# Another order for the last projection's blocks, and the MLP's second weight group in the place of finished rows: an encoder block on one core

## The chip, the core and the metric

The kernel runs on one core of a Trainium2 chip. A core has five engines with their own instruction queues: TensorE (PE) for matmuls, VectorE (DVE), ScalarE (ACT), GpSimd (POOL) and SyncE (SP), whose queue here holds nearly all DMAs. The metric is the time of one execution on the chip in microseconds; lower is better. Three timed runs of the kernel before took 1295.22, 1295.95 and 1296.48 us.

## What is computed

One layer of an encoder block on 1024 tokens of width 1024, in float32: RMSNorm, an input projection, neighbourhood attention and a gated short convolution, each with its own projection back, a gated sum of both called merged, and then these lines of the reference, which the change is about:

```python
x = x + merged @ w_o[l]
h = rms_norm(x, norm2_g[l]) @ w_mlp_in[l]       # 1024 x 4096
x = x + jnp.square(jax.nn.relu(h)) @ w_mlp_out[l]
```

## The kernel before

**Numbers.** Every float32 matmul is made of three fp16 ones: each operand is split into a high half and a low rest ("split" below: ACT copies the high half, DVE subtracts it from the operand), and three of the four products are added. High and low halves of the merged rows lie in tiles `M[0]` (mH) and `M[1]` (mL), the columns of one block of 128 tokens after those of another.

**The projection W_o.** `proj(b, half)` makes block b (128 tokens, eight of them) and half of the 1024 output columns: a group of 24 matmuls into one PSUM bank, then one DVE instruction that scales the bank and adds it into X1. Sixteen such groups; `anybank()` hands out eight banks in turn, so a later group waits for whoever reads the bank of the eighth before it. First come six half 0s (blocks 4, 5, 0, 1, 2, 6), then `built(cO[1])` waits for the weights of half 1, then the pairs: (0,1), (4,1), (1,1), (5,1), (3,0), (7,0), (2,1), (6,1), (3,1), (7,1).

**Pairs.** Blocks n and n+4 are a pair. When both halves of both are in X1, `pair(n)` makes their share of the MLP's input: squares and a reciprocal root for RMSNorm (ACT, DVE), a scaled copy of both blocks into a tile `form` (ACT), four differences and sums of these (`sums`, DVE), the split into `v16` (ACT, DVE), and two DMA transposes on SP's queue into U2[0] (u2T, forms 0 to 3) and U2[1] (u2x, forms 4 to 6).

**The MLP's first product.** It is done in seven products in place of eight (a two-by-two scheme in the manner of Strassen and Winograd), in 16 column groups q. `quad(q)` is one group: seven groups of 12 matmuls, one for each product, in the order 1, 6, 5, 4, 2, 7, 3; behind them the posts, small DVE additions from PSUM into the tile `as` (`post7`, for one, reads the banks of products 7, 4 and 5). Products 1, 2, 5 and 4 read u2T, and 6, 7 and 3 read u2x. Quads 0 and 1 run in two halves of 256 columns (256 tokens of each half of the tokens): first both first halves, which read the columns of pairs 0 and 1, and then both second halves, which read those of pairs 2 and 3. From quad 2 on the width is 512.

**Weights of a group.** For each q two raw tiles come by DMA; ACT scales them (`rows_scaled`, with the norm's gain), squares them for a power-of-two scale, POOL adds four form sums into `tsum` (`forms_sum`), a one-column matmul on PE adds up the squares over the partitions (`all_sum`; its column `ones` comes from DVE), and seven forms are split into fp16 into a tile `w16_1` (`forms_split`). These tiles take turns on three tags (`TAGS`); group 1's, "K", is the memory of the merged rows, so it waits for the last matmul of the projection. The prep of group q+1 starts when group q's split is out (L1206).

**What sets the order.** The program is written by generators: `fg` and `bg` are lists of foreground and background work. After each matmul group `unit(..., steps, ticks)` takes `steps` steps of the foreground and `ticks` steps of the background (L185). `need(q)` forces background until group q is ready. So steps, ticks and `gap`s decide behind which group each instruction stands. Each engine then works through its own queue in that order.

**W2.** After quad 15 the second product (weights again through the raw tiles of the same pool) starts: ACT squares its first weights, DVE reduces, POOL makes the sums of their forms; the squared-ReLU outputs `as` are turned into forms by POOL, stored by SP into HS and loaded again as `hf`.

## Time and profile before

| | us |
|---|---|
| profiled execution | 1298.12 |
| its span | 1296.0 |
| timed runs, median | 1295.95 |
| PE busy | 1217.8 (94% of the span) |
| DVE busy | 940.0 |
| ACT busy | 763.9 |
| POOL busy | 433.7 |

The span is the time from the first to the last instruction of the profiled execution, and all starts below count from it. Busy shares are averages: the projection, the quads and W2 have different limits, and so the prediction reads windows of the span and the waits of PE in them.

### The profile page before, as it was taken

To read this page: it belongs to the slowest core of one execution; us is meant where nothing else is said; L and a number is where in the kernel's file an instruction comes from. 1 tells how busy PE (TensorE), PEld (TensorE's weight loads), DVE (VectorE), ACT (ScalarE), POOL (GpSimd) and SP (SyncE) were. 2 spreads that over 40 slices of the span, in tenths; PEclk is the share of its full clock that TensorE was granted. 3 is DMA by queue.
4 is the path that set the end of the run, shared out by engine and by line. 5 is a ranking of instruction groups with operands and counts; after the bars stand their busy time and mean duration, and the time that the engine had idled before them with its cause. 6 is when DMAs were issued, how large, how long until landed. Compare 5 with 4: busy or idle time off the path is not lost. (4 is left out here: it accounts for less than half of the span.)

```text
span 1296.0 us, 17018 instructions
## 1 busy us (share of the span) xinstructions
PE 1217.8 (94%) x6294; PEld 579.5 (45%) x6294; DVE 940.0 (73%) x1719; ACT 763.9 (59%) x1169; POOL 433.7 (33%) x269
## 2 busy tenths in 40 slices
PE   5999997889999999999997899999996899999998
PEld 4544443444444444444456444444442344444443
DVE  7578767878657686886575476667746588889798
ACT  6777557667564455533665678777774564646430
POOL 2430011111231111100102587667738316080562
PEclk8999999989999999999998999999998899999999
DMA  6558445646552221225284454445462762526112
GB/s 251 125 196 159 106 70 118 132 81 139 113 112 84 65 65 37 70 86 193 63 165 104 147 179 140 151 157 179 170 228 90 240 239 92 234 98 244 67 64 98
DMA packets 170803, 173.35 MB, mean 134 GB/s; under 512 B 131424, under 2 KB 131936, under 8 KB 166624
## 3 DMA queue, kind: packets, MB, share of 16 engines
q1 hardware_dynamic: 170720, 172.27, 44.8%
q8 instruction: 49, 0.80, 0.3%
q14 instruction: 34, 0.28, 0.1%
HBM read 102.51 MB, written 37.75 MB: 108 GB/s over the span
## 5 line engine op out<-in xcount | busy, mean ns | idle before, releaser
L188 PEld LDWEIGHTS <-w 128*128 128x128 f16 x1512 | 149.7, 100 | 161.8 <-issue 9.8
L188 PEld LDWEIGHTS <-ops 128*128 128x128 f16 x1356 | 133.5, 99 | 181.3 <-issue 26.7
L1138 POOL TENSOR_TENSOR as<-as 128x512 f32<-128x512 f32 x64 | 111.7, 1746 | 85.3 <-ACT as L1271 81.6
L854 PE MATMUL ps_d<-uT,w_ws 128*128 128x512 f16 x528 | 128.3, 384 | 2.5 <-ACT w_ws L290 2.4
L188 PE MATMUL ps_s<-ops 128*128 128x512 f16 (+1 forms) x528 | 121.3, 380 | 7.1 <-ACT acc L1487 4.2
L188 PE MATMUL ps_d<-ops 128*128 128x512 f16 x492 | 115.4, 385 | 9.7 <-DVE as L1298 9.7
L188 PEld LDWEIGHTS <-uT 128*128 128x128 f16 x648 | 64.7, 100 | 70.7 <-issue 5.9
L1388 ACT ACTIVATE ops<-hf,sc 128x2048 f16<-128x2048 f32 x26 | 51.8, 1994 | 69.7 <-PE ps_d L188 24.7
L188 PE MATMUL ps_d<-u2T,w 128*128 128x512 f16 (+1 forms) x420 | 89.4, 365 | 3.3 <-DMA u2T<-v 2.9
L971 DVE SCALAR_TENSOR_TENSOR w<-raw,sc,w 128x512 f16<-128x512 f32 (+1 forms) x32 | 40.7, 1272 | 67.7 <-ACT w L977 67.7
L188 PEld LDWEIGHTS <-w_s 128*128 128x128 f16 x588 | 56.7, 98 | 71.3 <-DMA uT<-gs 2.2
L188 PE MATMUL ps_s<-u2x,w 128*128 128x512 f16 (+1 forms) x396 | 85.1, 366 | 3.2 <-DMA u2x<-v 3.2
L1390 DVE SCALAR_TENSOR_TENSOR ops<-hf,sc,ops 128x2048 f16<-128x2048 f32 x26 | 70.7, 2718 | 16.0 <-ACT ops L1388 16.0
L944 ACT ACTIVATE raw<-raw,sc 128x256 f32<-128x256 f32 x184 | 76.0, 494 | 6.1 <-DMA raw<-in_weights 6.1
L188 PE MATMUL ps_o<-ops 128*128 128x512 f16 x336 | 77.5, 380 | 1.4 <-DVE ops L1397 0.8
L958 POOL TENSOR_TENSOR tsum<-raw 128x512 f32<-128x512 f32 x30 | 50.8, 1710 | 81.2 <-ACT raw L944 66.3
L854 PEld LDWEIGHTS <-w_ws 128*128 128x128 f16 x528 | 51.1, 99 | 58.3 <-issue 3.9
L1403 POOL TENSOR_TENSOR raw<-raw 128x1024 f32<-128x1024 f32 x8 | 22.7, 2837 | 140.8 <-DVE ops L1397 140.8
L1269 ACT ACTIVATE as<-as 128x2048 f32<-128x2048 f32 x16 | 30.5, 1909 | 62.9 <-DVE as L1303 62.9
L958 POOL TENSOR_TENSOR gsum<-raw 128x512 f32<-128x512 f32 x14 | 18.5, 1338 | 133.4 <-issue 68.7
L971 DVE SCALAR_TENSOR_TENSOR w<-tsum,sc,w 128x1024 f16<-128x1024 f32 x30 | 61.4, 2087 | 0.0
L278 DVE SCALAR_TENSOR_TENSOR w_ws<-raw,sc,w_ws 128x512 f16<-128x512 f32 (+2 forms) x72 | 51.1, 764 | 3.5 <-ACT w_ws L290 3.5
(300 smaller groups left out, 2526.4 us busy)
## 6 DMA issues: line engine op xcount, KB each, us to landing
raw<-in_weights SPq DMA_DIRECT2D x92, 512.0 KB, 4.0
hs<-as SPq DMA_DIRECT2D x16, 1792.0 KB, 6.9
hf<-hs SPq DMA_DIRECT2D x26, 1024.0 KB, 10.4
w2x<-in_weights SPq DMA_DIRECT2D x16, 512.0 KB, 6.8
raw<-in_weights SPq DMA_DIRECT2D x16, 384.0 KB, 4.0
xt<-in_x SPq DMA_DIRECT2D x8, 512.0 KB, 9.8
gs<-s SPq DMA_DIRECT2D x4, 1024.0 KB, 6.6
x<-in_x SPq DMA_DIRECT2D x8, 512.0 KB, 8.6
```

The costliest lines, as they stand in the source:

```text
L188: T.matmul(ps, l, r, start=a, stop=b)
L278: V.scalar_tensor_tensor(lo, self.raw[p][:, o:o + m], sc[:, c:c + 1], hi, op0=OP.mult, op1=OP.subtract)
L854: T.matmul(ps, l, r, start=a, stop=b)
L944: A.activation(v, v, AF.Copy, scale=sc[:, at(g, 4 * i + k)])
L958: G.tensor_tensor(t[:, o], a, b, op=OP.add)
L971: V.scalar_tensor_tensor(P[:, a:b, 1], w, sc[:, s], P[:, a:b, 0], op0=OP.mult, op1=OP.subtract)
L1138: sub.tensor_tensor(z[o], z[a], z[b], op=op)
L1269: A.activation(f[:, 0:4], f[:, 0:4], AF.Relu)
L1388: A.activation(P[:, 1, 0], hf, AF.Copy, scale=sc[:, Rs])
L1390: V.scalar_tensor_tensor(P[:, 1, 1], hf, sc[:, Rs], P[:, 1, 0], op0=OP.mult, op1=OP.subtract)
L1403: G.tensor_tensor(w11[i2], w11[i2], w12[i2], op=OP.add)
```

## The change

It has five parts.

1. Half 0 of blocks 3 and 7 is moved behind pair 2. Pairs end at groups 8, 10, 12 and 16 in place of 8, 10, 14 and 16. Pair 3's squares are made in two halves, the first right behind (7, 0), and one DVE addition puts them together.
2. Group 1's weights are prepared by a function of their own, `prep_m`: six of the seven forms go into `M[0]`, into columns of blocks 0, 1, 2, 4, 5 and 6, whose groups have all been issued when `m_free` is set; the seventh goes into a small tile `t4`. The four sums are done by POOL in place, in the raw tiles, between the splits. Its work runs beside the projection's end, and group 1 needs no `tsum`. `seven` (its hunk is left out) now also takes a function that says where a form lies.
3. The background runs further ahead: `need(0)` in the projection is gone, ticks behind a half 1 group are 8, the gaps in `sums1` are shorter, and the chain of groups from 2 on follows right behind `prep_m`. From group 2 on, each group's `all_sum` and split stand about half a quad earlier.
4. Quads 0 and 1 take three foreground steps behind each group in place of two.
5. Their second halves run the products in the order 1, 2, 5, 4, 6, 7, 3 (those of u2T first), with post 5 behind post 6.

```diff
         ch.sum = sum_of(sm)
         yield
 
+    def parts(todo, s, then):
+
+        prev = None
+        for n, it in enumerate(todo + [None]):
+            if prev:
+                o, w = prev
+                V.scalar_tensor_tensor(o(1), w, sc[:, s], o(0), op0=OP.mult, op1=OP.subtract)
+                then(n - 1)
+            if it:
+                o, w = it
+                A.activation(o(0), w, AF.Copy, scale=sc[:, s])
+            prev = it
+            yield
+
     def forms_split(ch, t, s, P):
 
+        def then(n):
+            if n == 1:
+                done[0] += 2
+                load_upto(done[0] + 5)
         r = ch.r
         todo = [(0, 1, r[0][:, 0:1]), (1, 3, r[1]), (3, 5, t[:, 0:2]), (5, 7, t[:, 2:4])]
-        prev = None
-        for it in todo + [None]:
-            if prev:
-                a, b, w = prev
-                V.scalar_tensor_tensor(P[:, a:b, 1], w, sc[:, s], P[:, a:b, 0], op0=OP.mult, op1=OP.subtract)
-                if a == 1:
-                    done[0] += 2
-                    load_upto(done[0] + 5)
-            if it:
-                a, b, w = it
-                A.activation(P[:, a:b, 0], w, AF.Copy, scale=sc[:, s])
-            prev = it
-            yield
+        yield from parts([((lambda i, a=a, b=b: P[:, a:b, i]), w) for a, b, w in todo], s, then)
 
     def prep_s(n):
 
...
             sub.tensor_tensor(z[o], z[a], z[b], op=op)
             yield
 
-    pair_done, fv = [0], []
+    pair_done, fv, halves = [0], [], {}
+
+    def squares(n, half=None):
+
+        ss = tmp(2)
+        a, c = (8, slice(0, D)) if half is None else (4, slice(512 * half, 512 * half + 512))
+        for i in range(2):
+            A.activation(SQJ[:, :a], X1[:, n + 4 * i, c].rearrange("p (a t) -> p a t", a=a), AF.Square,
+                         accum_out=sc[:, at(ss, i)])
+        halves.setdefault(n, []).append(ss)
+        yield
 
     def pair(n):
 
-        ss, y = tmp(2), tmp(2)
-        for i in range(2):
-            A.activation(U2[1][:, 0, :, :, 384:512].rearrange("p s k t -> p (s k) t").bitcast(BF16),
-                         X1[:, n + 4 * i].rearrange("p (a t) -> p a t", a=8), AF.Square, accum_out=sc[:, at(ss, i)])
-        yield
-        yield from rstd(ss, D, y, 9)
+        y = tmp(2)
+        if n == 3:
+            yield from squares(3, 1)
+            a, b = halves[3]
+            V.tensor_tensor(sc[:, a], sc[:, a], sc[:, b], op=OP.add)
+        else:
+            yield from squares(n)
+            a = halves[n][0]
+        yield from rstd(a, D, y, 9)
         while pair_done[0] < n:
             yield
         if not n or n == 3:
...
     def sums1(q):
 
         ch = c1[q]
-        while q == 2 and pair_done[0] < 4:
-            yield
         if q == 0:
             tsum[0] = U2[1][:, 2].rearrange("p s k t -> p (s k t)").bitcast(F32).rearrange("p (i c) -> p i c", i=4)
-        elif q % 2:
+        elif q % 2 == 0:
+            while q == 2 and pair_done[0] < 4:
+                yield
             t = wsp.tile([128, 2, 4, 512], F32, name="tsum", tag="ws")
             for i in range(2):
                 tsum[q + i] = t[:, i]
         yield from rows_scaled(ch, g2)
-        yield from forms_sum(ch, tsum[q], 3 if q > 1 else 2 - q)
+        yield from forms_sum(ch, tsum[q], (0, 0, 1)[q] if q < 3 else 3)
 
     def prep1(q):
 
...
         P = P1[q] = pool.tile([128, 7, 2, 512], F16, name="w16_1", tag=tag)
         yield from forms_split(ch, tsum[q], s, P)
         ready.add(q)
-        if 0 < q < 15:
+        if 1 < q < 15:
             yield from sums1(q + 1)
+
+    SQJ = U2[1][:, 0, :, :, 384:512].rearrange("p s k t -> p (s k) t").bitcast(BF16)
+    m_free = [False]
+
+    def prep_m():
+
+        ch = c1[1]
+        yield from rows_scaled(ch, g2)
+        sm = cols_of("prep", 2)
+        for i in range(2):
+            A.activation(SQJ, ch.raw[i].rearrange("p (a t) -> p a t", a=8), AF.Square, accum_out=sc[:, at(sm, i)])
+            yield
+        ch.sum = sum_of(sm)
+        yield
+        s, ch.inv = yield from scale_of(ch.sum, 9, 3)
+        (w11, w12), (w21, w22) = ([ch.raw[i].rearrange("p (n m) -> p n m", n=2)[:, j] for j in range(2)]
+                                  for i in range(2))
+        while not m_free[0]:
+            yield
+        last = w4p.tile([128, 2, 512], F16, name="t4", bufs=1)
+
+        def place(f, n=1):
+            if f == 6:
+                return lambda i: last[:, i].rearrange("p (k c) -> p k c", k=4)
+            k, c = 4 * (f // 3), 128 * (f % 3)
+            return lambda i: M[0][:, k:k + 4, 512 * i + c:512 * i + c + 128]
+
+        def form(w):
+            return w.rearrange("p (k c) -> p k c", k=4)
+
+        def then(n):
+            if n < 4:
+                o, a, b = ((w11, w11, w12), (w12, w12, w22), (w22, w22, w11), (w21, w21, w22))[n]
+                G.tensor_tensor(o, a, b, op=OP.add)
+        yield from parts([(place(f), form(w)) for f, w in ((0, w11), (2, w22), (1, w21))], s,
+                         lambda n: then(n if n < 1 else 1) if n < 2 else (then(2), then(3)))
+        yield from parts([(place(f), form(w)) for f, w in ((3, w11), (4, w12), (5, w22), (6, w21))], s, lambda n: None)
+        done[0] += 2
+        load_upto(done[0] + 5)
+        P1[1] = lambda w, i, k: place(w)(i)[:, k]
+        ready.add(1)
+        yield from sums1(2)
 
 
     push(cO[1])
...
                 post()
         mm = tok_mms(ps, actM, b, cO[half], 8, 512, 0)
         if mms is None:
-            unit(mm, fin, 6, 4 + 2 * (half and b % 4 > 1))
+            unit(mm, fin, 6, 8 if half else 4)
         else:
             mms.append((mm, fin))
 
...
-    bg.extend([sums1(0), prep1(0)])
+    bg.extend([sums1(0), prep1(0), prep_m()])
+    bg.extend(prep1(q) for q in range(2, 16))
     two = []
     for b in (4, 5):
         proj(b, 0, None, two)
...
     for b in (0, 1, 2, 6):
         proj(b, 0)
     built(cO[1])
-    for n in range(4):
-        if n == 2:
-            proj(3, 0)
-            proj(7, 0)
-            need(0)
-            bg.append(sums1(1))
-            for q in range(1, 16):
-                bg.append(prep1(q))
+    for n in range(3):
         proj(n, 1)
         proj(n + 4, 1, lambda n=n: fg.append(pair(n)))
+    m_free[0] = True
+    proj(3, 0)
+    proj(7, 0, lambda: fg.append(squares(3, 0)))
+    proj(3, 1)
+    proj(7, 1, lambda: fg.append(pair(3)))
     pe_done[0] = 0
 
 
...
         ps = {}
         z = [AS[q][:, i, c0:c1] for i in range(7)]
 
+        def post6(ps):
+            V.tensor_tensor(z[5], ps[6], z[4], op=OP.add)
+            if c0:
+                post5(ps)
+
         def post5(ps):
             V.tensor_tensor(z[1], ps[5], z[5], op=OP.subtract)
 
...
                 fg.append(h_done(q))
         seven(P1[q], actU2, c0, c1, {
             1: lambda ps: A.activation(z[4], ps[1], AF.Copy),
-            6: lambda ps: V.tensor_tensor(z[5], ps[6], z[4], op=OP.add),
-            5: post5,
+            6: post6, 5: None if c0 else post5,
             2: lambda ps: V.tensor_tensor(z[0], ps[2], z[4], op=OP.add),
-            7: post7, 3: post3}, 2, 5)
+            7: post7, 3: post3}, 2 if c1 == 512 else 3, 5, (1, 2, 5, 4, 6, 7, 3) if c0 else (1, 6, 5, 4, 2, 7, 3))
 
     def whole(q):
         quad(q)
```

Three places in the instruction order. The first is DVE's queue from the projection's end into quad 0. Before, the last block of X1 (x1, from bank ps_s_6024) comes right behind pair 2's v16 subtractions (v16_5813, L1165), and group 1's split (w16_1_6085) behind that:

```order
L1165 TENSOR_TENSOR v16_5813<-form_5812,v16_5813 128x4x512
L1165 TENSOR_TENSOR v16_5813<-form_5812,v16_5813 128x3x512
L1226 SCALAR_TENSOR_TENSOR x1_5464<-ps_s_6024,sc_71,x1_5464 128x512
L390 TENSOR_SCALAR sc_71<-sc_71 128x2
L971 SCALAR_TENSOR_TENSOR w16_1_6085<-raw_5670,sc_71,w16_1_6085 128x512
L971 SCALAR_TENSOR_TENSOR w16_1_6085<-raw_5676,sc_71,w16_1_6085 128x2x512
L971 SCALAR_TENSOR_TENSOR w16_1_6085<-tsum_5932,sc_71,w16_1_6085 128x2x512 x2
```

Now pair 2's subtractions (v16_5831, L1185) stand among group 1's splits into the merged rows (mH_3618) and the small tile, and the last two blocks of X1 (banks ps_d_6013 and ps_s_6062) behind all of these:

```order
L969 SCALAR_TENSOR_TENSOR mH_3618<-raw_5676,sc_71,mH_3618 128x4x128
L1185 TENSOR_TENSOR v16_5831<-form_5830,v16_5831 128x4x512
L969 SCALAR_TENSOR_TENSOR mH_3618<-raw_5670,sc_71,mH_3618 128x4x128
L1185 TENSOR_TENSOR v16_5831<-form_5830,v16_5831 128x3x512
L969 SCALAR_TENSOR_TENSOR mH_3618<-raw_5670,sc_71,mH_3618 128x4x128
L969 SCALAR_TENSOR_TENSOR mH_3618<-raw_5676,sc_71,mH_3618 128x4x128
L969 SCALAR_TENSOR_TENSOR t4_6001<-raw_5676,sc_71,t4_6001 128x512
L1288 SCALAR_TENSOR_TENSOR x1_5464<-ps_d_6013,sc_71,x1_5464 128x512
L1288 SCALAR_TENSOR_TENSOR x1_5464<-ps_s_6062,sc_71,x1_5464 128x512
```

So four splits, which stood behind the last block, became seven, which stand in front of the last two. A little further on in the same queue are the posts of quad 0's first half (tile as_6068). Before, its post 7, which starts with the reading of bank ps_o_6165 at L1298, stands ahead of pair 3's two v16 subtractions (v16_6147):

```order
L1295 TENSOR_TENSOR as_6068<-ps_o_6116,as_6068 128x256
L1138 TENSOR_TENSOR form_6146<-form_6146 128x512 x2
L1310 TENSOR_TENSOR as_6068<-ps_s_6150,as_6068 128x256
L1138 TENSOR_TENSOR form_6146<-form_6146 128x512 x2
L1298 TENSOR_TENSOR as_6068<-ps_o_6165,as_6068 128x256
L1299 TENSOR_TENSOR as_6068<-ps_d_6132,as_6068 128x256
L1300 TENSOR_TENSOR as_6068<-ps_o_6116,as_6068 128x256
L1165 TENSOR_TENSOR v16_6147<-form_6146,v16_6147 128x4x512
L1303 TENSOR_TENSOR as_6068<-ps_d_6181,as_6068 128x256
L1165 TENSOR_TENSOR v16_6147<-form_6146,v16_6147 128x3x512
```

Now post 7 (tile as_6088, bank ps_o_6179, L1364) follows on both of pair 3's subtractions (v16_6141):

```order
L1356 TENSOR_TENSOR as_6088<-ps_s_6109,as_6088 128x256
L1145 TENSOR_TENSOR form_6140<-form_6140 128x512
L1361 TENSOR_TENSOR as_6088<-ps_o_6126,as_6088 128x256
L1145 TENSOR_TENSOR form_6140<-form_6140 128x512 x3
L1185 TENSOR_TENSOR v16_6141<-form_6140,v16_6141 128x4x512
L1375 TENSOR_TENSOR as_6088<-ps_s_6162,as_6088 128x256
L1185 TENSOR_TENSOR v16_6141<-form_6140,v16_6141 128x3x512
L1364 TENSOR_TENSOR as_6088<-ps_o_6179,as_6088 128x256
```

What moved are the posts against pair 3's work: before, both subtractions stood behind post 7; now both stand ahead of it.

The second place is PE's queue in quad 2. Before, the sum for group 4 (bank ps_o_6706) stands between quad 2's last product (weights w16_1_6396) and quad 3's first (w16_1_6602):

```order
L188 MATMUL ps_s_6690<-u2x_5485,w16_1_6396 128x512
L179 LDWEIGHTS ones_72
L179 MATMUL ps_o_6706<-ones_72 128x1
L188 LDWEIGHTS w16_1_6602
L188 MATMUL ps_d_6709<-u2T_5484,w16_1_6602 128x512
```

Now it (bank ps_s_6656) stands between two products of quad 2 (weights w16_1_6320), after the fourth:

```order
L188 MATMUL ps_d_6641<-u2T_5484,w16_1_6320 128x512
L179 LDWEIGHTS ones_72
L179 MATMUL ps_s_6656<-ones_72 128x1
L188 LDWEIGHTS w16_1_6320
L188 MATMUL ps_o_6659<-u2T_5484,w16_1_6320 128x512
```

The sum has moved from the border of two quads into the middle of one; the same holds for the later groups.

The third place is ACT's queue at the end of the quads. The tiles as_8168 and as_8313 of before belong to quads 13 and 14. Before, the split of group 15 (w16_1_8351) follows on quad 14's first copy (L1307), and W2's squares (L1357, L1360) on the split:

```order
L1307 ACTIVATE as_8313<-ps_d_8314 128x512
L977 ACTIVATE w16_1_8351<-raw_7920,sc_71 128x512
L977 ACTIVATE w16_1_8351<-raw_8063,sc_71 128x2x512
L977 ACTIVATE w16_1_8351<-tsum_8235,sc_71 128x2x512 x2
L1357 ACTIVATE h0_8380,sc_71<-raw_8065,sc_71 128x1024
L1357 ACTIVATE h0_8380,sc_71<-raw_8212,sc_71 128x1024
L1357 ACTIVATE h0_8380,sc_71<-raw_8214,sc_71 128x1024
L1357 ACTIVATE h0_8380,sc_71<-raw_8357,sc_71 128x1024
L1360 ACTIVATE h0_8380,sc_71<-w2x_8381,sc_71 128x2048 x2
L1269 ACTIVATE as_8313<-as_8313 128x2048
L1271 ACTIVATE as_8313,sc_71<-as_8313,sc_71 128x2048
```

Now group 15's split (w16_1_8297) stands ahead of quad 13's ReLU and square (as_8210, L1330 and L1332), and W2's squares (L1422, L1425) follow directly on quad 14's first copy (as_8340, L1373):

```order
L973 ACTIVATE w16_1_8297<-raw_7866,sc_71 128x512
L973 ACTIVATE w16_1_8297<-raw_8008,sc_71 128x2x512
L973 ACTIVATE w16_1_8297<-tsum_8030,sc_71 128x2x512 x2
L1330 ACTIVATE as_8210<-as_8210 128x2048
L1332 ACTIVATE as_8210,sc_71<-as_8210,sc_71 128x2048
L1373 ACTIVATE as_8340<-ps_d_8341 128x512
L1422 ACTIVATE h0_8356,sc_71<-raw_8010,sc_71 128x1024
L1422 ACTIVATE h0_8356,sc_71<-raw_8158,sc_71 128x1024
L1422 ACTIVATE h0_8356,sc_71<-raw_8160,sc_71 128x1024
L1422 ACTIVATE h0_8356,sc_71<-raw_8302,sc_71 128x1024
L1425 ACTIVATE h0_8356,sc_71<-w2x_8357,sc_71 128x2048 x2
L1330 ACTIVATE as_8340<-as_8340 128x2048
```

Between quad 14's copy and W2's squares stood four copies of a split; now nothing stands there.

More of the change, by code (lines that the diff above doesn't have):

```diff
@@ L1002, in seven @@
             post = posts.get(i)
-            unit(group(ps[i], [(P[:, w, sw, k * 128:k * 128 + 128], act(f, sa, k)[:, c0:c1])
+            unit(group(ps[i], [(at_w(w, sw, k), act(f, sa, k)[:, c0:c1])
                                for k in range(4) for sw, sa in PASSES]),
```

1 line of the change is left out of this document (added).

## The prediction

> **What bounds the kernel now.** I read the busy shares first, then a table of windows, then the waits of PE, then the timeline of each engine at the two places where PE waits.
>
> ```profile
> PE 1217.8 (94%) x6294; PEld 579.5 (45%) x6294; DVE 940.0 (73%) x1719; ACT 763.9 (59%) x1169; POOL 433.7 (33%) x269
> 662.00:680.00 18.00, 15.77 (x123) 12.51 (x122) 13.23 (x22) 11.97 (x15) 0.00 (x0) 0.91 0.86 167
> 680.00:700.00 20.00, 12.17 (x73) 8.75 (x73) 11.03 (x20) 9.70 (x17) 6.51 (x4) 0.77 0.57 123
> ...
> 760.00:900.00 140.00, 140.00 (x656) 63.56 (x655) 97.78 (x152) 108.03 (x160) 100.79 (x61) 1.00 0.45 155
> 955.00:1000.00 45.00, 34.16 (x148) 14.89 (x147) 23.89 (x27) 23.10 (x22) 26.72 (x10) 0.90 0.51 172
> ```
>
> In a row of windows stand the stretch, then the busy time of PE, PEld, DVE, ACT and POOL, then PE's granted clock. From 760 to 900 us PE is busy all 140 us at clock 1.00: there only fewer matmuls would help, and the change removes none. From 662 to 700 it idles 10 of 38 us and its clock falls to 0.77. PE loses time at two transitions: from the projection to the MLP's first quads (662 to 743), and from the last quads to W2 (955 to 1040).
>
> ```profile
> PE ps_o L179 <- DVE ones L925: 4.4, 2, 2.7
> PE ps_o L188 <- DVE as L1298: 4.0, 1, 4.0
> PE ps_s L188 <- DMA u2x<-v: 3.2, 2, 2.1
> PE ps_d L188 <- DMA u2T<-v: 2.9, 1, 2.9
> ```
>
> These are PE's waits from 655 to 765: 14.5 us. The timeline shows where they stand and what follows them:
>
> ```profile
> 662.51 1.47 PE L188 MATMUL ps_d<-u2T,w 128*128 128x256 f16 x12
> 666.08 2.12 PE L188 MATMUL ps_s<-u2x,w 128*128 128x256 f16 x12 [2.09 <-DMA u2x<-v]
> 668.00 2.53 PE L188 MATMUL ps_o<-u2T,w 128*128 128x256 f16 x12
> 670.36 1.47 PE L188 MATMUL ps_d<-u2T,w 128*128 128x256 f16 x12
> 671.67 1.47 PE L188 MATMUL ps_s<-u2T,w 128*128 128x256 f16 x12
> ...
> 683.88 2.72 PE L188 MATMUL ps_o<-u2T,w 128*128 128x256 f16 x12 [3.96 <-DVE as L1298]
> ...
> 693.78 2.53 PE L188 MATMUL ps_d<-u2T,w 128*128 128x256 f16 x12 [2.89 <-DMA u2T<-v]
> 697.37 2.72 PE L188 MATMUL ps_s<-u2x,w 128*128 128x256 f16 x12 [1.06 <-DMA u2x<-v]
> ...
> 717.90 0.16 PE L179 MATMUL ps_o<-ones 128*128 128x1 bf16 x1 [1.62 <-DVE ones L925]
> 717.92 2.75 PE L188 MATMUL ps_d<-u2T,w 128*128 128x512 f16 x12
> 720.51 2.75 PE L188 MATMUL ps_s<-u2x,w 128*128 128x512 f16 x12
> ...
> 738.94 0.16 PE L179 MATMUL ps_o<-ones 128*128 128x1 bf16 x1 [2.73 <-DVE ones L925]
> 738.97 4.15 PE L188 MATMUL ps_d<-u2T,w 128*128 128x512 f16 x12
> 742.95 2.32 PE L188 MATMUL ps_s<-u2x,w 128*128 128x512 f16 x10
> ```
>
> A group of 12 takes 1.31 us at half width (670.36 to 671.67) and 2.59 at full width (717.92 to 720.51). The 28 half-width groups of quads 0 and 1 would take 36.7; from 662.51 to 717.92 they took 55.4. Of the 18.7 lost, 11.6 are waits (2.09 + 3.96 + 2.89 + 1.06 + 1.62) and 7 are slow groups behind them: after the 3.96 wait the group lasts 2.72, not 1.47. Then 2.73 is lost at 738.94, and the group behind it needs 3.98 to its successor, 1.4 too much.
>
> **The change, step by step.** *Order of the projection.* The 16 groups and their matmuls stay. Pair 2 is complete two groups sooner, pair 3 still with the last group. Pair 2's transposes gate nothing PE waits for: the second halves of quads 0 and 1 need pair 3 as well.
>
> *The wait of 2.09.* Quad 0's second group waited for pair 1's u2x. In the new order group 0's weights are split before pair 1 is worked on, so SP reaches pair 1's transposes about 2.5 us sooner (it has only loads and transposes in its queue, in program order). Carried through, u2x lands at about 663.5, where PE wants it at 663.8. I count 2.1 of wait and 1.6 of slow clock (668.00 to 670.36 is 1.05 too long, 666.08 to 668.00 is 0.6 too long): **3.7 gained**; nothing at worst, if SP is no sooner.
>
> *Group 1's weights.* Before, they were split after the projection, in the idle stretch of DVE:
>
> ```profile
> 669.84 0.75 DVE L1226 SCALAR_TENSOR_TENSOR x<-ps_s,sc,x 128x512 f32<-128x512 f32 x1
> ...
> 684.53 2.28 DVE L1165 TENSOR_TENSOR v<-form,v 128x2048 f16<-128x2048 f32 x1
> ...
> 687.07 1.75 DVE L1165 TENSOR_TENSOR v<-form,v 128x1536 f16<-128x1536 f32 x1
> ...
> 730.02 0.75 DVE L971 SCALAR_TENSOR_TENSOR w<-raw,sc,w 128x512 f16<-128x512 f32 x1 [9.51 <-ACT w L977]
> 731.05 1.28 DVE L971 SCALAR_TENSOR_TENSOR w<-raw,sc,w 128x1024 f16<-128x1024 f32 x1 [0.29 <-ACT w L977]
> 732.26 2.47 DVE L971 SCALAR_TENSOR_TENSOR w<-tsum,sc,w 128x1024 f16<-128x1024 f32 x2
> ...
> 749.51 4.50 DVE L971 SCALAR_TENSOR_TENSOR w<-tsum,sc,w 128x1024 f16<-128x1024 f32 x2
> ```
>
> Seven single forms of 512 replace one of 512 and three of 1024. Seven at 0.75 are 5.3 us, against 0.75 + 1.28 + 2.47 = 4.5: 0.8 more on DVE, and as much on ACT. No row shows this split with 4x128 outputs; between 0.62 each (half of the 1024 row) and 1.13 each (half of the 749.51 row) it is 4.3 to 7.9. I take 5.3, the 512 form's own price nearby. What counts is where it stands: the seven splits and pair 2's v16 now come before the last two blocks of X1, which DVE takes from PSUM at about 671.6 and 672.4, not at 669.84. So PE's seventh group of quad 0, whose bank they free, waits about 1.9, and its slow clock costs 0.5: **2.4 lost**.
>
> *Pair 3.* Its half 0 is squared early, so behind the last evacuation come half a square and one small add, and not group 1's splits; I find its scale ready at 675.4, its forms on ACT to 677.6, its v16 on DVE from 681.4 to 685.8, not 684.53 to 688.8. Its transposes land about 3 sooner, near 690.7 and 694.1; PE's two DMA waits ended at 693.78 and 697.37.
>
> *Post 7 of quad 0.* With three foreground steps per group in place of two, both v16 subtractions of pair 3 go ahead of quad 0's L1364 on DVE. PE's fourth group of quad 1 waits for L1364's bank. PE would be there at 677.8 and goes on at about 686.2: a stall of 8.4 in place of 3.96, and 2.5 of slow clock behind it in place of 1.9: **5.0 lost**.
>
> *The second halves.* The three forms of u2T now come first and those of u2x last, so pair 3's u2x gets three groups of time. PE leaves the first halves at 686.2 + 2.5 + 4×1.31 = 693.9, where the 2.89, the 1.06 and their slow groups (1.2 + 1.2 + 0.5) were, and 14×1.31 = 18.3 follow without a wait; the 1.62 goes too, since its sum has moved forward. Quad 2 starts at **about 712.2 instead of 717.92: 5.7 gained**, all of the above included. With DVE stretched at its contended price it is 715; with L1364 two us earlier, 710.
>
> *The sums of group q.* From group 2 on each `all_sum` stands in the middle of a quad, not at its end. The 2.73 at 738.94 and the 1.4 behind it go: **4.1 gained**. What hides the sum then are three groups, 7.8 us; if its ones were late again it would cost the old 2.73. First transition: 9.8; I take **9**, for POOL's four added sums beside DVE.
>
> A rule and a row on the clock: in the windows above the granted clock is 0.91 around a wait of 2.09. The Trainium skill, "TensorE: Matmul & The Clock Gate", section "Why this matters for your kernels", wants no gaps over about 3 us, as if shorter ones cost only themselves. The group at 668.00 shows 2.53 after 2.09, so the trace does not agree. By the rule alone the slow groups behind the short waits (1.6 + 2.9 + 1.4) could not be counted, and the transition would give 3, the whole 1288.
>
> *The end of the quads.* Here the same earlier phase acts on W2's start:
>
> ```profile
> 945.08 7.36 POOL L1138 TENSOR_TENSOR as<-as 128x512 f32<-128x512 f32 x4 [4.72 <-ACT as L1271]
> 969.93 8.28 POOL L1138 TENSOR_TENSOR as<-as 128x512 f32<-128x512 f32 x4 [17.48 <-ACT as L1271]
> ...
> 953.57 1.15 ACT L1357 ACTIVATE h<-raw,sc 128x1024 bf16<-128x1024 f32 x1 [4.35 <-DVE w L971]
> ...
> 962.92 0.16 DVE L924 TENSOR_REDUCE sc<-sc 128x1 f32<-128x6 f32 x1 [7.39 <-ACT h L1360]
> ...
> 995.48 5.28 PE L188 MATMUL ps_d<-ops 128*128 128x512 f16 x12 [9.72 <-DVE as L1298]
> ...
> 1025.94 0.59 PE L188 MATMUL ps_s<-ops 128*128 128x512 f16 x1 [4.16 <-ACT acc L1487]
> ...
> raw<-in_weights SPq DMA_DIRECT2D x92, 512.0 KB, 4.0
> ```
>
> (The last line is of the page's DMA issues, with 4.0 us from issue to landing.) POOL's form sums come every 7×2.59 = 18.1 us, one quad; those of quad 14 were due at 963.2 and came at 969.93, 6.7 late: W2's squares on ACT began at 953.57, DVE stood 7.39 with the reduction behind them, until 962.92, and quad 14's posts behind that. Group 15's split now stands half a quad sooner, so its raw buffers, W2's loads and the squares may start at about 945.5, right behind the copy of quad 14's first group. Then DVE's reduction is past at 955 and POOL is on time. Its whole chain (L1403, L1404, L1408) moves by up to 6.7, and with it the end of the 9.72 wait; the 2.5 of slow clock behind that stays. The 4.16 at 1025.94 moves along with quad 15's stored forms. Bounds: 0, if W2's loads are no sooner, and 6.7. I take **5**.
>
> **Sum.** 9 + 5 = 14. The profiled execution took 1298.12, with 2.1 around its span of 1296.0: it would take 1284. The median of the runs is 1295.95, 2.2 below the profiled one, so I predict 1295.95 − 14 = **1282**.
>
> **Rivals.** *Only the first transition.* W2's start may hang on its DMAs and not on the ACT order: then 9 alone, 1287. For it: the 953.57 row names DVE's split as the releaser, with loads between; against: the loads follow that split by about 4 us of 8.
>
> *DVE's queue eats the first part.* Pair 3 and L1364 end no sooner than before, and only the 4.1 of the later sums (or part of it) is left: 1292 to 1295. For it: DVE is busy 13.23 of 18 us from 662 on, and now gets more.
>
> *Slower: POOL's sums in place.*
>
> ```profile
> L958 POOL TENSOR_TENSOR tsum<-raw 128x512 f32<-128x512 f32 x30 | 50.8, 1710 | 81.2 <-ACT raw L944 66.3
> ```
>
> The four forms still to be split wait for POOL's adds, which wait for the first three; DVE's evacuations of X1 stand behind all seven. DVE and POOL stretch each other: 2.47 for two splits beside an idle POOL (732.26), 4.50 beside a busy one (749.51). Four adds at 1.7 are 6.8; were they and the splits stretched alike by 1.8, 6.8 + 5.3 become 22, 10 more. The delay reaches PE twice, at the bank and at L1364. From a delay of 9.8 on the first transition gains nothing; with 12 to 14, and W2 as before, 1298 to 1300. Against it: DVE has pauses in this stretch that take up part of it.
>
> The Trainium skill, "SBUF — State Buffer", section "Who interferes with whom", says that a DVE instruction with two SBUF inputs contends with a GpSimd one that reads SBUF, and that the one behind is held for the whole instruction. The rows at 732.26 and 749.51 agree (1.8 times). It speaks against these sums; serialised strictly, only 6.8 would be added and the result would be about 1289.
>
> *More gained.* If post 7 gets ahead of one v16 subtraction, the 8.4 stall is 4 or less: 1275.
>
> *It does nothing of the kind.* If group 1's weights waited for the last reader of the merged rows all the same, their split would end where it did. The finished blocks are read last at group 12, so this is 0.01 and I add it to the second rival.
>
> **How the numbers follow.** Chances: the forecast 0.58 (1277 to 1285), only the first transition 0.15, DVE's queue 0.12, slower 0.09, more gained 0.06. The range, 1273 to 1296, takes in the bounds 0 to 6.7 of the W2 term, the 2 to 3 either way of quad 2's start and the second rival; it leaves out the slower case and half of the larger gain. About 0.2% is what a measurement here can tell from no change: 1293.4 to 1298.5. Half of the second rival lies in it, so faster is 0.58 + 0.15 + 0.06 + 0.06 = 0.85, the same 0.06, slower 0.09.
>
> **What would show it.** The 2.09 wait gone; a wait of about 8 on L1364 near 678 to 686; no DMA waits in the second halves; quad 2 starting near 712 and no wait on L925 afterwards; quads 2 to 13 at 18.13 each; ACT's first W2 square within 1 us of quad 14's copy, POOL's sums of quad 14 on time, the 9.72 at 4 to 5. The forecast is wrong if X1's last evacuation comes after 676, if quad 2 starts after 716, or if W2's squares still wait for data.

## The result, and the profile after

The changed kernel takes 1282.58 us (median of 4 runs, 1282.23 to 1283.73) where the kernel before takes 1296.22: a ratio of 0.9894, 95% interval 0.9877 to 0.9911. Predicted were 1282.0. Of all runs below, two took 2122.39 us (the change without the phase) and 2538.50 us (the last but one below), far from every other run of the same kernel, and they are left out of the medians. The profiled spans are 1296.0 before and 1280.1 after, 15.9 apart.

To see where these 15.9 went, I cut the span at the starts of four groups of matmuls on PE that both kernels have. A ends where the first half-width MLP group starts (662.51 before), B where quad 2's first group does (717.92), C where W2's first product does (976.86), D where the first product in a ps_o bank behind the long wait there does (1003.48), and E with the span:

| us | A, to the end of the projection | B, quads 0 and 1 | C, quads 2 to 15 | D, start of W2 | E, rest | span |
|---|---|---|---|---|---|---|
| before | 662.51 | 55.41 | 258.94 | 26.62 | 292.52 | 1296.0 |
| after | 661.21 | 52.20 | 254.15 | 20.48 | 292.06 | 1280.1 |
| gained | 1.3 | 3.2 | 4.8 | 6.1 | 0.5 | 15.9 |
| predicted | 0 | 5.7 | 4.1 | 5 for D and E | | 14 (14.8, less 0.8 kept back for POOL's sums) |

A is hardly a gain of the change: a kernel below that shares this whole stretch with the changed one has 663.34, and over all of them it lies anywhere from 660.90 to there. B scatters too: the two kernels below that differ from the changed one only from quad 8 on have 52.66 and 52.71 in place of 52.20, so half a microsecond in B says nothing. First B, in PE's waits from 640 to 760, and then in its timeline (start, duration, instruction, and in brackets the idle time ahead and its releaser):

```profile
PE ps_o L188 <- DVE as L1364: 6.2, 1, 6.2
PE ps_d L188 <- DVE x L1288: 5.1, 1, 5.1
```

```profile
661.21 1.47 PE L188 MATMUL ps_d<-u2T,w 128*128 128x256 f16 x12
662.52 1.47 PE L188 MATMUL ps_s<-u2x,w 128*128 128x256 f16 x12
...
674.35 2.74 PE L188 MATMUL ps_d<-u2x,w 128*128 128x256 f16 x12 [5.11 <-DVE x L1288]
676.88 2.12 PE L188 MATMUL ps_s<-u2T,mH 128*128 128x256 f16 x12
...
687.87 2.72 PE L188 MATMUL ps_o<-u2T,t 128*128 128x256 f16 x12 [6.25 <-DVE as L1364]
...
713.41 2.75 PE L188 MATMUL ps_d<-u2T,w 128*128 128x512 f16 x12
...
721.18 0.17 PE L179 MATMUL ps_s<-ones 128*128 128x1 bf16 x1
```

The wait of 2.09 for u2x is gone, and so are the DMA waits of 2.89 and 1.06 and the 1.62. In their place stand 5.11 for a bank that the last blocks of X1 leave late, and 6.25 for post 7, each with slow groups behind it. DVE's and POOL's timelines show why the first is so long:

```profile
658.38 0.75 DVE L969 SCALAR_TENSOR_TENSOR mH<-raw,sc,mH 128x512 f16<-128x512 f32 x1
659.05 0.68 DVE L1145 TENSOR_TENSOR form<-form 128x512 f32<-128x512 f32 x1
659.66 1.76 DVE L969 SCALAR_TENSOR_TENSOR mH<-raw,sc,mH 128x512 f16<-128x512 f32 x1
661.34 3.43 DVE L1145 TENSOR_TENSOR form<-form 128x512 f32<-128x512 f32 x2
...
666.01 2.28 DVE L1185 TENSOR_TENSOR v<-form,v 128x2048 f16<-128x2048 f32 x1
668.21 1.76 DVE L969 SCALAR_TENSOR_TENSOR mH<-raw,sc,mH 128x512 f16<-128x512 f32 x1
...
673.55 0.73 DVE L1288 SCALAR_TENSOR_TENSOR x<-ps_d,sc,x 128x512 f32<-128x512 f32 x1
674.22 0.73 DVE L1288 SCALAR_TENSOR_TENSOR x<-ps_s,sc,x 128x512 f32<-128x512 f32 x1
```

```profile
659.21 5.01 POOL L1270 TENSOR_TENSOR raw<-raw 128x512 f32<-128x512 f32 x3 [41.42 <-DVE mH L969]
666.23 3.19 POOL L1270 TENSOR_TENSOR raw<-raw 128x512 f32<-128x512 f32 x1 [2.01 <-DVE mH L969]
```

A split takes 0.75 before POOL's sums begin and 1.76 beside them; a form sum 0.68 and 1.72. X1's last blocks leave PSUM at 673.55 and 674.22.

C and D go as predicted in kind. After 713.41 PE does not wait until W2. (The sum for group 4 starts at 721.18, three groups of 2.59 after 713.41: it stands behind quad 2's third product, and not behind the fourth, as was said where its place in the queue was shown.) At the end of the quads, on POOL, ACT and PE:

```profile
936.31 5.33 POOL L1145 TENSOR_TENSOR as<-as 128x512 f32<-128x512 f32 x4 [12.84 <-ACT as L1332]
954.45 8.11 POOL L1145 TENSOR_TENSOR as<-as 128x512 f32<-128x512 f32 x4 [12.81 <-ACT as L1332]
```

```profile
936.14 0.58 ACT L1373 ACTIVATE as<-ps_d 128x512 f32<-128x512 f32 x1
936.62 1.14 ACT L1422 ACTIVATE h<-raw,sc 128x1024 bf16<-128x1024 f32 x1
```

```profile
980.43 5.19 PE L188 MATMUL ps_d<-ops 128*128 128x512 f16 x12 [4.94 <-DVE as L1364]
...
1009.99 0.59 PE L188 MATMUL ps_s<-ops 128*128 128x512 f16 x1 [3.65 <-ACT acc L1552]
```

W2's first square follows directly on quad 14's copy, POOL's sums of quad 14 come 18.1 after those of quad 13, on time, and the wait of 9.72 is 4.94.

### The profile page after: what moved, and what is told of

Same layout as the page of the kernel before. It is cut to its first block, busy times and chain, and to the rows that moved or that the text cites. A ratio compares the mean times of both kernels' runs of the same rounds, so it can differ in the third digit from the quotient of the medians.

```text
span 1280.1 us, 17022 instructions
## 1 busy us (share of the span) xinstructions
PE 1211.6 (95%) x6294; PEld 578.2 (45%) x6294; DVE 917.8 (72%) x1723; ACT 765.7 (60%) x1176; POOL 406.7 (32%) x269
## 5 line engine op out<-in xcount | busy, mean ns | idle before, releaser
L188 PEld LDWEIGHTS <-w 128*128 128x128 f16 x1344 | 131.0, 98 | 145.0 <-DVE x L1288 5.4
L188 PE MATMUL ps_d<-u2T,w 128*128 128x512 f16 (+1 forms) x504 | 111.8, 371 | 0.0
L1145 POOL TENSOR_TENSOR as<-as 128x512 f32<-128x512 f32 x64 | 89.9, 1405 | 58.6 <-ACT as L1332 54.9
L188 PE MATMUL ps_s<-u2x,w 128*128 128x512 f16 (+1 forms) x360 | 80.0, 372 | 0.0
L958 POOL TENSOR_TENSOR tsum<-raw 128x512 f32<-128x512 f32 x28 | 39.6, 1424 | 70.1 <-ACT raw L944 70.1
L973 ACT ACTIVATE w<-raw,sc 128x512 f16<-128x512 f32 (+1 forms) x30 | 26.4, 927 | 46.5 <-DVE sc L410 46.5
L188 PEld LDWEIGHTS <-mH 128*128 128x128 f16 x400 | 39.5, 100 | 32.3
L290 ACT ACTIVATE w_ws<-raw,sc 128x512 f16<-128x512 f32 (+2 forms) x72 | 40.9, 636 | 19.9 <-DVE sc L253 19.9
```

What stands on the lines that cost most here:

```text
L188: T.matmul(ps, l, r, start=a, stop=b)
L290: A.activation(self.parts[:, 0, f + o:f + o + m], self.raw[p][:, o:o + m], AF.Copy, scale=sc[:, c:c + 1])
L958: G.tensor_tensor(t[:, o], a, b, op=OP.add)
L973: A.activation(o(0), w, AF.Copy, scale=sc[:, s])
L1145: sub.tensor_tensor(z[o], z[a], z[b], op=op)
```

## The experiments

The question was which of the five parts makes which piece. Times are medians where not said otherwise; the ratio is to the kernel before on the same chip, with its 95% interval. All letters are those of the table above, each read from one profile.

**The phase alone, in the kernel before.**

```diff
-        yield from forms_sum(ch, tsum[q], 3 if q > 1 else 2 - q)
+        yield from forms_sum(ch, tsum[q], (2, 1, 0)[q] if q < 3 else 3)
```

> The kernel before with one number changed: the gap of group 2's sums is 0 in place of 3, so that from group 2 on each sum stands in the middle of a quad; projection, group 1 and quads 0 and 1 stay as before. Theory (the phase alone makes the gain of the quads' sums, 4.1, and of the end of the quads, 6): waits on L925 gone, POOL's sums of quad 14 on time, time 1285 to 1288, that is three quarters of the whole gain. Rival (the gain hangs together with group 1's weights in the merged rows; alone, the earlier sums collide with pair 3 on DVE): the waits at quads 0 and 1 grow by 4 or more, time 1291 to 1296.

1284.95 us, ratio 0.9892 (0.9868 to 0.9916): as much as the whole change, within what can be told. B 52.59, C 254.15, D 20.91, E 292.42. PE's waits from 655 to 765, and POOL at the end of the quads:

```profile
PE ps_d L179 <- DVE ones L925: 5.0, 1, 5.0
PE ps_o L188 <- DVE as L1298: 4.0, 1, 4.0
PE ps_s L188 <- ACT v L1163: 2.1, 1, 2.1
```

```profile
937.73 5.32 POOL L1138 TENSOR_TENSOR as<-as 128x512 f32<-128x512 f32 x4 [12.84 <-ACT as L1271]
955.85 8.11 POOL L1138 TENSOR_TENSOR as<-as 128x512 f32<-128x512 f32 x4 [12.81 <-ACT as L1271]
```

Three waits of 11.0 us, against 11.4 in two with the whole change. In B group 2's sum now stands among the first halves and costs 5.0 there, but pair 3's transposes have landed by the time PE goes on: the waits on them are gone. C and D are those of the changed kernel.

**The change without the phase.**

```diff
-        yield from forms_sum(ch, tsum[q], (0, 0, 1)[q] if q < 3 else 3)
+        yield from forms_sum(ch, tsum[q], (0, 0, 4)[q] if q < 3 else 3)
```

> The changed kernel without its earlier phase: group 2's gap is 4 in place of 1, so that each sum from there on stands at the border of two quads, at the same place of PE's queue as in the kernel before; projection order, group 1's path, steps and product order stay changed. Theory (the phase alone is the gain, after the run in which one gap in the kernel before gave 13 us): the sums' waits, 4 to 5 us, and the late POOL sums at the end, 6 us, are back; time 1292 to 1296. Rival (the other parts give half of it as well, and the two overlap): 1286 to 1290.

1297.74 us, ratio 1.0012 (1.0000 to 1.0024): nothing left of the gain, and 1.7 above what was expected. B is 52.68, 2.7 better than before, but C is 262.07 and D 25.49. On PE and on POOL:

```profile
738.50 0.16 PE L179 MATMUL ps_o<-ones 128*128 128x1 bf16 x1 [4.79 <-DVE ones L925]
738.52 5.23 PE L188 MATMUL ps_d<-u2T,w 128*128 128x512 f16 x12
...
996.09 4.45 PE L188 MATMUL ps_d<-ops 128*128 128x512 f16 x12 [9.71 <-DVE as L1364]
```

```profile
945.72 7.36 POOL L1145 TENSOR_TENSOR as<-as 128x512 f32<-128x512 f32 x4 [4.38 <-ACT as L1332]
970.55 8.28 POOL L1145 TENSOR_TENSOR as<-as 128x512 f32<-128x512 f32 x4 [17.48 <-ACT as L1332]
```

The sum at the border of quads 2 and 3 waits 4.79 (2.73 before): what quads 0 and 1 finish sooner is waited for there. And POOL's sums of quad 14 are late again (24.8 after quad 13's). These two runs settle the main question from both sides.

**The phase later from quad 8 on.** To part C from D, one gap in the middle was lengthened: to 6, which put the sum ahead of a quad's last product, and then, with 7 in the same line, to the border.

```diff
-        yield from forms_sum(ch, tsum[q], (0, 0, 1)[q] if q < 3 else 3)
+        yield from forms_sum(ch, tsum[q], (0, 0, 1)[q] if q < 3 else 6 if q == 8 else 3)
```

> The gap of group 8's sums is 6 in place of 3: from quad 8 on every group's preparation stands about half a quad later again, as in the kernel before; quads 0 to 6 are untouched. Theory (the gain at the end of the quads comes from this phase alone): no wait up to quad 14, POOL's sums of quad 14 are again 6 to 7 us late, the wait of 4.94 on DVE as L1364 grows to 9 to 10, and the time is 1287 to 1290. Rival (the gain there comes from the shorter use of raw tiles or from group 1's other path): unchanged, 1282 to 1284.

1299.68 us, ratio 1.0011 (0.9997 to 1.0026), 9.7 above what was expected. D and E together lose 4.6 against the changed kernel (317.14 for 312.54; the long wait is 9.67), but C is 264.96: the sum waits 0.7 to 1.7 us in each of seven quads, 9.7 in all, 7.8 of it put down to `ones`. The groups behind these waits keep their 2.59. The 9.7 belong to this one place of the sum, so the time of this run did not tell the theories apart.

> As the run with group 8's gap at 6, but at 7, so that from quad 8 on each sum stands exactly at the border of two quads, as in the kernel before; at 6 it stood ahead of a quad's last product and PE waited 1 to 2 us for it in each of five quads (9.6 in all). Theory (the phase makes the gain at the end of the quads): no such waits within the quads (under 2 us in all, quads 8 to 13 at 18.1), POOL's sums of quad 14 late again, 26 us in place of 20.5 from W2's first product to the end of the slow group behind the long wait; 6 us lost, time 1287 to 1290. Rival (quads with the later sums lose by themselves, so the end is not what counts): waits within the quads as before, time above 1292.

1290.81 us, ratio 0.9952 (0.9935 to 0.9969). C is 254.64 and PE waits 0.4 in it; D and E together are 319.40, where the kernel before has 319.14 and the changed one 312.54. So the end of the quads is worth 4.6 (from the run before) to 6.9, by the phase there alone; the time is 0.8 above what was expected. Over all fourteen profiles D and E together take 317.14 to 320.02 in the four kernels with the later phase at the end of the quads, and 311.74 to 314.26 in the ten with the earlier one. Most of it is D, 24.52 to 26.62 against 19.33 to 21.19; E lies between 290.77 and 294.93, without an order by the phase.

**The projection's old order.**

```diff
-    for n in range(3):
+    for n in range(2):
         proj(n, 1)
         proj(n + 4, 1, lambda n=n: fg.append(pair(n)))
-    m_free[0] = True
     proj(3, 0)
     proj(7, 0, lambda: fg.append(squares(3, 0)))
+    proj(2, 1)
+    proj(6, 1, lambda: fg.append(pair(2)))
+    m_free[0] = True
```

> All of the changed kernel, but the projection's second halves in the old order: pairs end at groups 8, 10, 14 and 16, and group 1's weights may go to the merged rows from group 14 on. From the projection's end to quad 2 the changed kernel takes 52.2 us, the kernel before 55.4. Theory (the order gives little, since the second halves wait for pair 3 in both): 52 to 54, time 1282 to 1285. Rival (pair 2 two groups sooner is what makes room on DVE): 56 to 58, time 1287 to 1289.

1285.38 us, 0.4 above what was expected, with a ratio of 0.9918 (0.9903 to 0.9933), which overlaps the changed kernel's; B is 53.32 against 52.20 (52.66 and 52.71 in the profiles of the two runs above). The new order is worth 0.6 to 1.1 us in B, little, as the theory gave it, and not clear of B's scatter.

**Two steps, and the old order of products, in quads 0 and 1.**

```diff
-            7: post7, 3: post3}, 2 if c1 == 512 else 3, 5, (1, 2, 5, 4, 6, 7, 3) if c0 else (1, 6, 5, 4, 2, 7, 3))
+            7: post7, 3: post3}, 2, 5, (1, 2, 5, 4, 6, 7, 3) if c0 else (1, 6, 5, 4, 2, 7, 3))
```

> Quads 0 and 1 take two foreground steps again, so quad 0's post 7 stands ahead of both of pair 3's v16 subtractions on DVE. Theory (these three steps are a trade: they delay post 7 and bring pair 3's transposes forward): the wait on L1364 falls from 6.25 us to about 2 (post 7 would end near 683), but pair 3's transposes come about 1.5 us later and the second halves wait for u2T for 2 to 4 us; quad 2 starts between 712 and 715, the time is 1281 to 1285. Rival (post 7 alone sets the time of quads 0 and 1): quad 2 starts 4 us sooner, near 709, and the time is about 1278.

1285.35 us, ratio 0.9901 (0.9877 to 0.9925), at the upper end of what was expected. The wait on L1364 (post 7) falls from 6.25 to 0.6, as post 7 now stands ahead of pair 3's subtractions, and B to 50.68. But all sums move one product later, and PE waits 3.4 in B and 2.1 in C for `ones`; C is 257.00. The trade is there, though it is paid in sums and not in u2T, which was my expectation.

The second edit puts the old order of products back; post 5 goes back behind product 5 with it (its lines are left out here).

```diff
-            7: post7, 3: post3}, 2 if c1 == 512 else 3, 5, (1, 2, 5, 4, 6, 7, 3) if c0 else (1, 6, 5, 4, 2, 7, 3))
+            7: post7, 3: post3}, 2 if c1 == 512 else 3, 5, (1, 6, 5, 4, 2, 7, 3))
```

> The second halves of quads 0 and 1 run their products in the old order, u2x second. Theory (the new order gives pair 3's u2x transpose the time it needs): with u2T landed at about 692 and u2x at about 695.5 against a second half that starts at 695.05, hardly a wait is left: 0 to 1 us, time 1282 to 1284. Rival (the order is what removed the waits of 2.89 and 1.06): both come back with their slow groups, 4 to 7 us, time 1287 to 1290.

1283.78 us, ratio 0.9888 (0.9861 to 0.9915), B 53.03 and no DMA wait at all. With the rest of the change in place the order of the products takes no wait away.

**POOL's sums left out.** The four in-place sums are dropped, so that group 1's last four forms are those of unsummed weights.

```diff
-            if n < 4:
-                o, a, b = ((w11, w11, w12), (w12, w12, w22), (w22, w22, w11), (w21, w21, w22))[n]
-                G.tensor_tensor(o, a, b, op=OP.add)
+            return
```

> The changed kernel without POOL's four sums of group 1's raw tiles; group 1's last four forms are therefore left unsummed. Theory (POOL's sums stretch DVE's splits and pair 2's subtractions and so make 3 to 4 of the 5.11 us on L1288): those instructions fall to their short durations (0.75 in place of 1.76, 0.7 in place of 1.7), the last evacuation of X1 ends 3 to 5 us sooner, the wait on L1288 is 0.5 to 2; from the projection's end to quad 2 49 to 51 us in place of 52.2. Rival (the evacuations are late by their place behind the splits alone): wait 4 to 5, 52 us.

One run, 1279.65, with B 49.08. On DVE:

```profile
660.97 0.75 DVE L969 SCALAR_TENSOR_TENSOR mH<-raw,sc,mH 128x512 f16<-128x512 f32 x1
661.63 1.41 DVE L1145 TENSOR_TENSOR form<-form 128x512 f32<-128x512 f32 x2
...
664.28 2.28 DVE L1185 TENSOR_TENSOR v<-form,v 128x2048 f16<-128x2048 f32 x1
...
670.80 0.75 DVE L1286 SCALAR_TENSOR_TENSOR x<-ps_d,sc,x 128x512 f32<-128x512 f32 x1
```

The same split that took 1.76 takes 0.75, the two form sums 1.41 in place of 3.43. Counted from the projection's end (662.53 here, 661.21 there), X1's last blocks leave PSUM 4.1 sooner, and the wait of 5.11 is gone altogether, where 0.5 to 2 was expected. So POOL's sums cost B 3.1 us. Pair 2's large subtraction takes 2.28 either way. In neither kernel does DVE stand idle from the second of these splits to X1's last block, so no split waited for a sum of POOL: 1.0 for this split, 2.0 for the two form sums and 1.0 for the split at 668.21 are the 4.1, all of it stretch beside POOL.

**A later split, and combinations.** One background step behind the projection's last two groups puts the evacuations of X1 ahead of the four late splits.

```diff
-            unit(mm, fin, 6, 8 if half else 4)
+            unit(mm, fin, 6, (1 if m_free[0] else 8) if half else 4)
```

> The changed kernel with one background step, in place of eight, behind the projection's last two groups, so that the last two blocks of X1 stand on DVE ahead of the four late splits of group 1. Theory (the wait of 5.11 us on L1288 and the late pair 3 come from these evacuations standing behind splits that wait for POOL): both evacuations about 4 us sooner, the 5.11 falls to 0.5 to 1.5, post 7 ends near 683.5 in place of 687.8; 48 us from the projection's end to quad 2 in place of 52.2; time 1278 to 1280. Rival (pair 3 is held by the contention of DVE with POOL whatever the order, or the late splits now hold quad 1): 51 to 53 us, time 1282 to 1284.

1282.40 us, ratio 0.9897 (0.9880 to 0.9913), B 50.84: the rival's time, and 2.4 above the theory's. On PE:

```profile
671.71 1.48 PE L188 MATMUL ps_d<-u2x,w 128*128 128x256 f16 x12 [1.17 <-DVE x L1288]
...
687.06 2.72 PE L188 MATMUL ps_o<-u2T,t 128*128 128x256 f16 x12 [8.73 <-DVE as L1364]
```

The 5.11 falls to 1.17 as expected, but post 7 hardly comes sooner, and most of the time saved is waited for at L1364: 8.73 for 6.25. DVE's queue shows why, from the first of the small steps that make pair 3's scale (L1166) to the last (L399):

```profile
673.26 0.16 DVE L1166 TENSOR_TENSOR sc<-sc 128x2 f32<-128x2 f32 x1 [0.29 <-ACT u2x L1155]
...
673.87 0.75 DVE L969 SCALAR_TENSOR_TENSOR mH<-raw,sc,mH 128x512 f16<-128x512 f32 x1 [0.25 <-ACT mH L973]
...
676.31 0.16 DVE L399 SCALAR_TENSOR_TENSOR sc<-sc 128x2 f32<-128x2 f32 x1
```

These steps start at 673.26 and the last of them at 676.31, with three of the late splits among them; in the changed kernel they start at 675.89 and 677.12. Counted from the projection's end the first comes 2.6 sooner, and the last only 0.8. The 1.4 gained in B cannot be told from no change in the time.

With two steps besides:

```diff
-            7: post7, 3: post3}, 2 if c1 == 512 else 3, 5, (1, 2, 5, 4, 6, 7, 3) if c0 else (1, 6, 5, 4, 2, 7, 3))
+            7: post7, 3: post3}, 2, 5, (1, 2, 5, 4, 6, 7, 3) if c0 else (1, 6, 5, 4, 2, 7, 3))
```

> As the run with one background step behind the last two groups, and two foreground steps in quads 0 and 1, so that post 7 of quad 0 also stands ahead of pair 3's v16. Theory: no stall over 2 us on L1364, as with two steps alone (0.62), but group 2's and 3's sums come late as they did there (5.5 us on L925); 47 to 49 us from the projection's end to quad 2, and 1 to 3 lost after it; time 1279 to 1282, no better than one step alone. Rival (the gains add): 1275 to 1277.

1284.90 us, ratio 0.9914 (0.9898 to 0.9929), 2.9 above what was expected: B 49.66, C 258.68. The 2.5 us won in quads 0 and 1 are more than given back, 4.5, behind quad 2's start, where the sums stand one product later.

With group 2's gap 0 on top of both, the sums are back in their place:

```diff
-        yield from forms_sum(ch, tsum[q], (0, 0, 1)[q] if q < 3 else 3)
+        yield from forms_sum(ch, tsum[q], 0 if q < 3 else 3)
```

> The version with all that the runs so far favour: one background step behind the projection's last two groups, two foreground steps in quads 0 and 1 (post 7 ahead of pair 3's v16), and group 2's gap 0 in place of 1, which puts the sums back to the changed kernel's place behind the fourth product; with gap 1 they stood one product later and 4.5 us were lost after quad 2. Theory: 49 to 50.5 us from the projection's end to quad 2, 254.2 from there to W2, time 1279 to 1281. Rival (the earlier sums bring back the wait on L925 among the first halves): 51 to 53 us, 1282 to 1284.

1286.08 us, ratio 0.9919 (0.9897 to 0.9941): C is 254.14 as it should be, but B is 52.85, with 5.35 waited for group 2's `ones`; in B the rival was right, though the time lies 2.1 above even its range. E is 294.93, 2.9 longer than in the changed kernel, with 7.25 on L1552 where that has 3.65; I have no cause for that.

With one background step and this same gap, but three steps as in the changed kernel, the phase is one product earlier than there.

> One background step behind the projection's last two groups, and the phase a group earlier still: group 2's gap 0, sums behind the third or second product. Theory (the gain at the end comes from group 15's split being early enough; the W2 squares follow directly on quad 14's copy already, so no more is to be had): 254.2 us for the quads, 20 to 20.5 behind W2's first product, group 2's sum collides with pair 3 on DVE for 1 to 3 us; time 1280 to 1284. Rival (each group of phase gives another 1.5 us at the end): 1277 to 1279.

1293.74 us, ratio 0.9980 (0.9971 to 0.9989): dearer than either theory gave. D is 20.35, so nothing more is to be had there, as the theory said; but group 2's sum waits 12.08 us behind pair 3, and B is 55.01 and C 263.10, with 6.1 on L925 (`ones`) after quad 2's start:

```profile
689.30 0.16 PE L179 MATMUL ps_s<-ones 128*128 128x1 bf16 x1 [12.08 <-DVE ones L925]
```

None of these that does the same work beats the changed kernel clearly.

## Why the prediction was right, and where its working was not

The time, 1282.58 for 1282.0, is right, and so are the signs. By its steps:

- *The 2.09 wait*: gone in the changed kernel's profile, but with little to spare: in four of the runs that keep this part PE waits 1.15 to 1.22 at the same group.
- *Group 1's splits ahead of X1's last blocks*: right in kind, **the wrong size**. I took 5.3 us for seven splits, the price without POOL, and a wait of 1.9; it was 5.11, and with its slow groups some 7 were lost where I had 2.4. The run without POOL's sums shows the missing part, 3.1 us of B, and its B of 49.08 is close to what I had forecast (712.2 − 662.5 = 49.7), with a stall of 8.03 at post 7 where I had 8.4. The rival of POOL's sums named the mechanism, with a factor of 1.8 where these instructions show 2.3 to 2.5; X1's last blocks were 4.1 late by it, not the 9.8 from which it would have decided.
- *Post 7*: predicted to end the stall at 686.2, measured 687.87; the stall is 6.25 and not 8.4 only because PE arrived later. Two steps take it away, and the time does not fall.
- *The second halves without waits*: right, but I put it down to pair 3 and the order of the products. The order of products is not needed for it, nor the merged rows: with the phase alone these waits are gone as well. Pair 3's subtractions ended at 687.49, where I had 685.8, and still nothing waited for its transposes.
- *The later sums, 4.1*: measured 4.8. *The end of the quads, 5*: measured 6.6 (D and E), by the steps named: split half a quad sooner, squares behind the copy, POOL on time.
- *The sum* came out so close by luck: B's gain was forecast 2.5 too high and those of C and the end 2.3 too low together, and these errors cancel; 1.3 more lies in A, in the profile alone (the runs' medians are 13.6 apart). The 5.7 for B came from a chain of start times. The single gains and losses named on the way (3.7, −2.4, −5.0, the second halves' 2.89, 1.06 and 2.9, and 1.62) add up to 4.8, which is nearer to the 3.2 measured.

What the prediction did not see is that its parts do not add. It worked out 9.1 for the phase and 4.9 for the rest (with the 1.62, which is the phase's, counted in the rest). One gap in the kernel before gives 0.9892, and all the rest without the phase 1.0012. In B each side by itself gains 2.7 to 2.8 and both together 3.2 (2.7 in the two profiles that share B with the changed kernel), since quads 0 and 1 wait for DVE's queue in any case and only the place of the waits moves; and without the phase the B that the rest gains is waited for again at the border of quads 2 and 3.

## What to carry to other kernels

When a steady loop is bound by one engine, the phase at which its background work runs can be free in the loop and still decide how its ends fit: look there before restructuring the work, and try the one number that shifts it, in both directions. It is not free everywhere: here one product earlier cost 11 us, one later 3 to 4.5 behind quad 2's start (part of which quads 0 and 1 gave back), and a sum ahead of a quad's last product 9.7 within the loop. Price an instruction by the row taken beside the same neighbours, not by the row next to it. And of a change in several parts, undo the cheapest one alone and do it alone: here these two runs told most of it.

## What was not expected of the hardware

The phase parts DVE's splits from POOL's sums in every quad. Instructions of DVE in 745 to 930, grouped by shape, before and then after (count, busy us and mean ns):

```profile
L971 DVE SCALAR_TENSOR_TENSOR w<-tsum,sc,w 128x1024 f16<-128x1024 f32 x20 | 45.0, 2290 | 0.0
```

```profile
L969 DVE SCALAR_TENSOR_TENSOR w<-tsum,sc,w 128x1024 f16<-128x1024 f32 x22 | 27.2, 1277 | 0.0
```

and the window of steady quads after the change (busy PE, PEld, DVE, ACT, POOL, then the clock):

```profile
760.00:900.00 140.00, 140.00 (x657) 63.54 (x655) 79.45 (x149) 108.72 (x160) 79.09 (x62) 1.00 0.50 166
```

DVE falls from 97.78 to 79.45 us and POOL from 100.79 to 79.09 with the same work, and PE, busy throughout in both, takes no less. It is slack, not time. That it is the phase is shown by the same window in the two runs that part it from the rest: with the phase alone DVE has 80.55 and POOL 80.19, with all but the phase 97.72 and 100.05, and the mean of the split is 1277 and 2289 ns. (The Trainium skill, "SBUF — State Buffer", section "Who interferes with whom", has this contention for a DVE instruction with two SBUF inputs beside a GpSimd one that reads SBUF; here it is a factor of 1.8 for the 1024-wide split and of 2.3 for the 512-wide one beside the projection. That the one that starts first is not held, as the section says, also agrees: POOL's last sum begins at 666.23, behind a 2.28 us subtraction of DVE that keeps its duration, and takes 3.19.)

PE's slow groups have a rough border in these runs. Behind waits of 0.97, 1.17, 1.22 and 1.69 us the next half-width groups take their 1.47, and behind the seven of 0.67 to 1.70 in the run with gap 6 the full-width ones keep their pace; behind 2.06, 2.09, 2.51 and 2.52 one of the next two half-width groups takes 2.5 to 2.8. (The 1.06 of the kernel before, with 2.72 behind it, comes 3.6 us after a wait of 2.89.) The border is not sharp: behind a wait of 2.10 for group 4's sum in quad 2, the next group took 2.75, as usual, with two steps alone, and 4.44 with one background step besides. So a wait of two us can cost more than one and a half times itself (the 2.06 cost 3.7 in all), and where it does, cutting it to 1.2 saves both.
